# Six gather buffers in place of eight, two more kept weight units a layer, and diagonals that hold the gates ahead, in a hybrid decoder trunk on one core

## The chip, the core and the metric

The kernel runs on one core of one Trainium2 chip. It computes the whole trunk in one launch. The metric is the device time of that launch in microseconds. Before the change the median of three runs is 3154.29 us (3154.21 to 3155.14). The profile was taken of one further execution, which took 3156.79 us.

## The reference

Four layers work on 256 tokens of 1024 features in float32. The token mixers are HGRN2, FoX, Mamba-2 SSD and HGRN2 again. Behind each mixer stands a PEER expert block, which is where most of the bytes are:

```python
def peer_ffn(h, w_q, sub_keys, u_tab, v_tab):
    ...
        q = (xb @ w_q).reshape(M, PEER_HEADS, 2, PEER_HALF)
        s = jnp.einsum('mhcd,hckd->mhck', q, sub_keys).astype(jnp.float32)
        sv, si = lax.top_k(s, PEER_TOPK)
        ...
        top_s, pos = lax.top_k(cand_s, PEER_TOPK)
        idx = jnp.take_along_axis(cand_i, pos, axis=-1)
        gates = jax.nn.softmax(top_s, axis=-1)
        u = jnp.take(u_tab, idx, axis=0)
        v = jnp.take(v_tab, idx, axis=0)
        act = jax.nn.gelu(jnp.einsum('md,mhkd->mhk', xb, u).astype(jnp.float32), approximate=False) * gates
        return jnp.einsum('mhk,mhkd->md', act.astype(xb.dtype), v)
```

For each token, 8 heads choose 16 of 16384 experts each. An expert is a row `u` (dotted with the token) and a row `v` (added to the output with weight gelu(dot) times gate).

## The kernel before

The 256 tokens are two tiles of 128. A layer's expert block on one tile is a **stage**, so there are 8 stages (`STAGES`). A stage has 8 heads, a head has 8 **pairs** (`NQ`), so a stage has 64 pairs and the program 512 (`pairs`). A pair is two gathers: each brings 128 rows of `uv`, a row being 1024 values of u and 1024 of v, which is 1 MiB, into one of `NGB` buffers `GB[...]`. The two gathers of pair i are numbers 2i and 2i+1, and number n goes to `GB[n % NGB]`. In the last stage (numbers from `LAST` on) there are more buffers, the list `END`: `GB` and pieces of the memory of the weights, which are done by then.

One pair's way through the engines, in program order (the loop from L1514):

- `fetches(i)`: POOL issues gathers as indirect DMAs (L1359), as long as their row numbers are known and fewer than 2i + `NGB` are sent. A gather waits until the last reader of its buffer, TensorE's products of `NGB`/2 pairs earlier, is done.
- `dot(i, 0)`, `dot(i, 1)`: VectorE multiplies the u half with the tokens (`XR`) and sums, one number a row, into the tile `dots`.
- `spread(i)`: ScalarE computes Gelu of the two columns, multiplies each by its gate (`got[s, hh][1]`, the tile `gs`), and multiplies the mask `m64` (128 x 64, shown as `m_82`) by each result, which makes two diagonals `dg`. TensorE multiplies each diagonal with the two v halves of its buffer and adds to the accumulators `acc` (L1410): 4 calls, which are 8 matmul instructions in the trace.
- `route_steps`: VectorE, with an Exp on ScalarE, does a few steps of choosing the rows of later heads.
- `products_` and `others`: a piece of the side work `side(s)`, which is the mixer, norms and query projection of the next tile. Its calls are woven between the pairs, with costs reckoned at build time. The last of a stage's side work is drained at pair 62.

Stage s works on tile s % 2 of layer s // 2, and its side work makes ready stage s + 1. So the side work of stages 0, 2, 4, 6 is the second tile's pass over a layer, and that of 1, 3, 5 the first tile's pass over the next layer. The first pass of layer 0 runs alone ahead of the stages.

Weights come as **units** of 128 x 2048 values (1 MiB) by DMAs of SP's queue (`loads`, L354), in the order of use. Units named in `EARLY` and `LATE` have a place of their own in the memory `mix` (`place`): they are loaded for the first tile only, and the second tile finds them there. All other units are loaded for both tiles, into one of two buffers `raw` (`NRAW`). `EARLY` and `LATE` together name 11, 10, 10 and 11 units for the four layers: 42. `mix` is as long as its largest layer needs. In the lone first pass, `homes` gives some units of layer 0 a place in memory that isn't needed yet, gather buffers among it; a gather into such a buffer waits until the unit has been used.

Of the kernel before, what the change touches and what calls it, by code (L numbers as in the profile page):

```python
# [10 lines left out]
F32 = mybir.dt.float32  # L11
# [4 lines left out]
AF = mybir.ActivationFunctionType  # L16
# [3 lines left out]
P = 128  # L20
T = 256
D = 1024
# [4 lines left out]
HALF = UNIT // 2  # L27
TOPK = 16
NQ = TOPK // 2
NGB = 8  # L30
NRAW = 2
STAGES = 2 * DEPTH

KIND = ("hg", "fox", "ssd", "hg")
EARLY = {"hg": (0, 2, 4, 5, 8, 12), "fox": (0, 4, 8, 2, 10), "ssd": (0, 4, 8, 6, 29)}
LATE = {"hg": (25, 19, 21, 23, 27), "fox": (17, 19, 21, 12, 14), "ssd": (33, 35, 37, 39, 26)}
SOON = {"hg": (19, 21), "fox": (), "ssd": ()}
NEXT = {"hg": (), "fox": (12, 14), "ssd": (26,)}
# [1 line left out]
TURN = 8 * 131  # L40
MIX = max((len(EARLY[k]) + len(LATE[k])) * UNIT + MIDDLE[k] for k in MIDDLE)

# [127 lines left out]
def trunk(ctx: ExitStack, tc: tile.TileContext, d: dict, out: bass.AP):  # L170
# [4 lines left out]
    wk2 = ctx.enter_context(tc.tile_pool(name="wk2", bufs=2))  # L175
# [10 lines left out]
    sizes = (("h0", TURN), ("h1", TURN), ("xT", D), ("XR", 2 * D), ("keys", UNIT), ("SS", 2048), ("mix", MIX),  # L186
             ("gb", NGB * 2 * D))
    arena = cpool.tile([P, sum(n for _, n in sizes)], F32, name="arena")
    at_, o_ = {}, 0
# [5 lines left out]
    XR = at_["XR"].rearrange("p (g n) -> p g n", g=2)  # L195
    keys = at_["keys"].rearrange("p (g k) -> p g k", g=16)
    SS = at_["SS"].rearrange("p (h c k) -> p h c k", h=8, c=2)
    GB = [at_["gb"][:, i * 2 * D:(i + 1) * 2 * D] for i in range(NGB)]
    mix = at_["mix"]
# [17 lines left out]
    def act(o, i, f, **k):  # L217

        if f not in ghosts:
            table[0] = f  # L220
        nc.scalar.activation(o, i, f, **k)  # L221
# [15 lines left out]
    m64 = cpool.tile([P, 64], F32, name="m64")  # L237
# [13 lines left out]
    def hidden(s):  # L251

        return HB[(s - 1) % 2 if s else 0][:, 0:D]
# [5 lines left out]
    def middle(kind):  # L259

        at = [len(EARLY[kind]) * UNIT]
        most = MIX - len(LATE[kind]) * UNIT
# [8 lines left out]
    def outer(kind, t):  # L271

        at = [0 if t else MIX - len(LATE[kind]) * UNIT]
        most = len(EARLY[kind]) * UNIT if t else MIX

# [7 lines left out]
    def place(l, i):  # L283

        kind = KIND[l]
        if i in EARLY[kind]:
            o = EARLY[kind].index(i) * UNIT
        elif i in LATE[kind]:
# [5 lines left out]
    def bank():  # L294
        return psp.tile([P, 512], F32, name="ps")
# [5 lines left out]
    for l in range(DEPTH):  # L301
        nm = ("hg%d" % (l // 3), "fox", "ssm", "hg%d" % (l // 3))[l]
        n = UNITS[KIND[l] if KIND[l] != "ssd" else "ssm"]
        for t in range(2):
# [1 line left out]
            stream += [("wq%d" % l, i) for i in range(8)]  # L306
            places += [(t, l, i, place(l, i)) for i in range(n + 8)]

    homes = {1: GB[0], 3: GB[1], 6: GB[2], 7: GB[3], 9: GB[6], 10: GB[7], 11: at_["SS"], 13: at_["XR"], 16: GB[0],
             17: GB[1], 18: GB[2], 20: GB[3], 22: GB[7]}  # L310
    order = [0, 1, 2, "rest", 3, 4, 5, 6, 7, 8, 9, 10, 11, 12, 13, 14, 15, 16, 17, 18, 20, 22, "keys", "factors", 19, 21,
             24, "heads", 23, 25, "states", 26, 27]
    asked = {("early", 0), ("soon", 0), ("late", 0), ("next", 0)}
    for u in range(28, len(stream)):
        t, l, i, where = places[u]
        if where is not None and not t:
            k = KIND[l]
            token = ("early" if i in EARLY[k] else "soon" if i in SOON[k] else "next" if i in NEXT[k] else "late"), l
            if token not in asked:
# [818 lines left out]
    scored, got, routed = set(), {}, [0]  # L1138
# [206 lines left out]
    pairs = [(s, hh, q) for s, hh in heads for q in range(NQ)]  # L1345
    acts = {}
# [1 line left out]
    sent = [0]  # L1348

    LAST = 2 * NQ * 8 * (STAGES - 1)  # L1350
    END = GB + [mix[:, o:o + 2 * D] for o in range(3 * D, MIX - 2 * D + 1, 2 * D)]

    def buffer(n):

        return GB[n % NGB] if n < LAST else END[(n - LAST) % len(END)]

# [5 lines left out]
    def known(i):  # L1362

        s, hh, _ = pairs[i]
        return got[s, hh][2] if (s, hh) in got else 0

    def fetches(n):

        while sent[0] < 2 * len(pairs) and pairs[sent[0] // 2][2] < known(sent[0] // 2):
            if sent[0] - LAST >= NGB and 2 * n < LAST:  # L1370
                return
            if sent[0] >= 2 * n + (len(END) if sent[0] - LAST >= NGB else NGB):
                return
# [2 lines left out]

    def dot(i, g):
        if g == 0:
            acts[i] = wk2.tile([P, 3, 2], F32, name="dots", bufs=4)
        u = buffer(2 * i + g)[:, 0:D]  # L1380
        stt(u, u, 1.0, XR[:, g], op0=OP.mult, op1=OP.mult, accum_out=acts[i][:, 0, g:g + 1])

    def warm(n, b, x):

        for _ in range(n):
            nc.tensor.matmul(b, x[:, 0:P], x[:, 0:512], start=True, stop=True)

    def begin(s):

        accs[s] = [accp.tile([P, 512], F32, name="acc") for _ in range(2)]  # L1390
        for e in range(2):
            nc.tensor.matmul(accs[s][e], ident, hidden(s)[:, e * 512:(e + 1) * 512], start=True, stop=False)

    def spread(i):
        s, hh, q = pairs[i]
        a = acts.pop(i)
        dg = wk2.tile([P, 2, 64], F32, name="dg", bufs=4)
        act(a[:, 1], a[:, 0], AF.Gelu)
        for g in range(2):
            act(a[:, 2, g:g + 1], a[:, 1, g:g + 1], AF.Copy, scale=got[s, hh][1][:, g, 1, q:q + 1])  # L1400
        for g in range(2):
            act(dg[:, g], m64, AF.Copy, scale=a[:, 2, g:g + 1])
        if s and hh == 0 and q == 0:
            begin(s)
        if i == len(pairs) - 1:
            warm(3, bank(), cst)
        for e in range(2):
            for g in range(2):
                v = buffer(2 * i + g)[:, D + e * 512:D + (e + 1) * 512]
                nc.tensor.matmul(accs[s][e][g * 64:g * 64 + 64], dg[:, g], v, start=False,  # L1410
                                 stop=hh == 7 and q == NQ - 1)


    mixers = {"hg": hgrn, "fox": fox, "ssd": ssd}
# [75 lines left out]
    for s in range(STAGES):  # L1490
# [23 lines left out]
        for i in range(64 * s, 64 * s + 64):  # L1514
            new, end = i % 64 == 0 and s > 0, i % 64 == 63 and s + 1 < STAGES
            fetches(i)
            dot(i, 0)
            if end:
                for o, b in x[:2]:
                    nc.scalar.copy(o, b)  # L1520
            elif new:

                products_(True)
                others()
            dot(i, 1)
            spread(i)
            if end:
                (_, b), (o, c) = x[2:]
                nc.scalar.copy(x[2][0], b)
                vec.tensor_copy(o, c)  # L1530
            route_steps(3 if i > 3 else 5, i // 8 + 3)
            others()
            products_()
            if i % 64 == 62 and s + 1 < STAGES:
                while not state["done"]:
                    others()
                    products_(True)
                others()
                x = repeated()
            if table[0] is not AF.Gelu:  # L1540
                act(spare, eps, AF.Gelu)
# [20 lines left out]
```

## Time and profile before

| | before |
|---|---|
| median of three runs | 3154.29 us |
| the profiled execution | 3156.79 us |
| its span, first to last instruction | 3155.0 us |
| busy: PE, DVE, ACT, POOL | 78%, 67%, 43%, 38% of the span |
| mean granted clock of TensorE | 0.918 |
| read from HBM | 1288.38 MB |

The page gives busy times of each engine, a line with the bytes per second in 40 equal slices of the span, the DMA queues (q0 carries the gathers, q1 the weights), the chain of work that ended last, and groups of instructions by line and tile, with their number, busy time, mean duration and the idle time ahead of them. Answers of the trace add the same for a stretch of time (windows), or the instructions in order of time (timeline; in square brackets the idle time ahead of an instruction and what ended it). The 16 DMA engines' share of busy time stands behind the granted clock in a windows row.

### The profile page before, as it was taken

Reading aid. Unit: us, or ns where it says so; the run is one execution under the profiler, and the core shown is the slowest. Engines: PE = TensorE matmul, PEld = TensorE weight load, DVE = VectorE, ACT = ScalarE, POOL = GpSimd, SP = SyncE. Lnnn points to the kernel's source line nnn. Section 1 sums busy time; section 2 is a strip of 40 time slices with the busy share of each in tenths; the row PEclk is TensorE's granted clock in tenths of the full one; section 3 lists DMA queues with packets and bytes.
Section 4 is the critical chain, followed back from the end, with each engine's and each line's share of the span. In section 5 each row is a group of like instructions: output and inputs, shape, how many; then the busy total and the mean of one; then the engine's idle time right before and its main releaser. Section 6 shows DMA issues by size and latency. Waiting matters only on the chain.

```text
span 3155.0 us, 30986 instructions
## 1 busy us (share of the span) xinstructions
PE 2473.3 (78%) x8674; PEld 1104.9 (35%) x8674; DVE 2111.0 (67%) x5589; ACT 1362.1 (43%) x3911; POOL 1199.6 (38%) x1032
## 2 busy tenths in 40 slices
PE   9988787777778786888788988878767788775565
PEld 4433333333333433344233443333323333332222
DVE  2576757576676766778557887476665767577764
ACT  2344424353343533477334764245432553333332
POOL 0234334333443443333233333343433444345443
PEclk9999998988899998999889998989989998998877
DMA  8799999999999999999999999999999999999997
GB/s 338 285 421 421 421 421 411 421 420 420 411 420 420 402 421 403 422 421 421 412 418 416 418 411 408 421 418 420 421 409 421 409 419 403 421 421 421 421 422 322
DMA packets 178729, 1291.48 MB, mean 409 GB/s; under 512 B 19840, under 2 KB 20608, under 8 KB 21632
## 3 DMA queue, kind: packets, MB, share of 16 engines
q0 software_dynamic: 147456, 1073.81, 82.4%
q1 hardware_dynamic: 31104, 215.70, 16.6%
q8 instruction: 72, 1.18, 0.2%
q14 instruction: 97, 0.79, 0.1%
HBM read 1288.38 MB, written 1.05 MB: 409 GB/s over the span
## 4 chain that ended last, share of the span: by engine, by line
DMA 59%; PE 16%; DVE 12%; issue 6%; ACT 4%; POOL 2%; POOLq 0%; SPq 0%; DVEq 0%; ACTq 0%
DMA arena<-in_uv,ix 59%; DVE arena L208 9%; PE acc L1410 8%; PE pj L243 5%; PE ps L243 3%; POOL arena L1359 2%; ACT dots L221 2%; ACT L221 1%; DVE cs L208 1%; ACT dg L221 1%; ACT arena L221 1%; PE ps L247 0%; DVE si L208 0%; DVE af L208 0%; DVE sv L208 0%
## 5 line engine op out<-in xcount | busy, mean ns | idle before, releaser
L1359 POOL DMA_INDIRECT arena<-in_uv,ix x1024 | 1195.5, 1168 | 1925.6 <-PE acc L1410 1345.9
L208 DVE SCALAR_TENSOR_TENSOR arena<-arena 128x1024 f32<-128x1024 f32 (+3 forms) x1282 | 1319.9, 1048 | 827.9 <-DMA arena<-in_uv,ix 775.7
L1410 PE MATMUL acc<-arena,dg 128*64 128x512 f32 x4096 | 1255.8, 693 | 651.5 <-ACT dg L221 637.2
L1410 PEld LDWEIGHTS acc<-arena,dg 128*64 128x64 f32 x4096 | 473.9, 150 | 1258.1 <-ACT dg L221 959.9
L221 ACT ACTIVATE dots<-dots 128x2 f32<-128x2 f32 x512 | 103.3, 202 | 1563.9 <-DVE arena L208 1552.2
L243 PE MATMUL pj<-raw,arena 128*128 128x512 f32 x1144 | 554.5, 617 | 6.9 <-DMA raw<-in_fox 3.7
L221 ACT ACT_TABLE_LOAD x331 | 424.7, 1283 | 7.0 <-DVE arena L208 0.8
L243 PE MATMUL pj<-arena 128*128 128x512 f32 (+1 forms) x792 | 368.6, 602 | 3.9 <-DMA arena<-in_hg 1.7
L243 PEld LDWEIGHTS pj<-raw,arena 128*128 128x128 f32 x1144 | 204.5, 193 | 344.2 <-issue 313.4
L221 ACT ACTIVATE dg<-m,dots 128x64 f32<-128x64 f32 x1024 | 292.4, 332 | 0.0
L221 ACT ACTIVATE dots<-dots,gs 128x1 f32<-128x1 f32 x1024 | 245.6, 286 | 16.8
L243 PEld LDWEIGHTS pj<-arena 128*128 128x128 f32 x792 | 142.9, 192 | 214.0 <-issue 199.9
L243 PE MATMUL ps<-arena 128*128 128x128 f32 (+6 forms) x1088 | 139.4, 285 | 1.5 <-issue 0.8
L243 PEld LDWEIGHTS ps<-arena 128*128 128x128 f32 (+3 forms) x1088 | 113.6, 171 | 72.2 <-issue 44.4
L247 PEld LDWEIGHTS ps<-fst,arena 128*128 128x128 f32 x568 | 69.7, 149 | 83.4 <-issue 49.0
L247 PE MATMUL ps<-fst,arena 128*128 128x128 f32 x568 | 92.3, 291 | 5.6 <-ACT ig L221 3.3
L208 DVE DVE_READ_ACCUMULATOR arena<-arena 128x1 f32 x1024 | 84.2, 82 | 0.0
L221 ACT ACTIVATE arena<-arena 128x512 f32<-128x512 f32 (+3 forms) x130 | 66.4, 553 | 40.6 <-DVE arena L208 38.3
L208 DVE FIND_INDEX8 si<-sv,arena 128x8 uint32<-128x128 f32 x256 | 69.8, 285 | 0.0
L243 PE MATMUL ps<-cst,arena 128*128 128x128 f32 (+3 forms) x288 | 69.0, 367 | 0.0
L208 DVE MAX8 sv<-arena 128x8 f32<-128x128 f32 x256 | 61.6, 282 | 5.8 <-ACT arena L1177 5.7
L221 ACT ACTIVATE arena<-ps 128x512 f32<-128x512 f32 (+3 forms) x114 | 43.4, 426 | 33.1 <-PE ps L243 32.5
(122 smaller groups left out, 1259.0 us busy)
## 6 DMA issues: line engine op xcount, KB each, us to landing
raw<-in_ssm SPq DMA_DIRECT2D x52, 1024.0 KB
raw<-in_hg SPq DMA_DIRECT2D x41, 1024.0 KB
raw<-in_wq SPq DMA_DIRECT2D x32, 1024.0 KB
arena<-in_hg SPq DMA_DIRECT2D x25, 1024.0 KB
raw<-in_fox SPq DMA_DIRECT2D x18, 1024.0 KB
arena<-in_wq SPq DMA_DIRECT2D x17, 1024.0 KB
arena<-in_uv,ix POOLq DMA_INDIRECT x1024
arena<-in_fox SPq DMA_DIRECT2D x7, 1024.0 KB
```

The source lines that it names most:

```text
L208: return getattr(nc.vector, name)(o, *a, **k)
L221: nc.scalar.activation(o, i, f, **k)
L243: nc.tensor.matmul(o, w, m, start=start, stop=stop)
L247: nc.tensor.transpose(o, i, ident)
L1359: nc.gpsimd.indirect_dma_start(buffer(n), None, d["uv"], bass.IndirectOffsetOnAxis(ap=got[s, hh][0][:, g, q:q + 1], axis=0))
L1410: nc.tensor.matmul(accs[s][e][g * 64:g * 64 + 64], dg[:, g], v, start=False, stop=hh == 7 and q == NQ - 1)
```

## The change

- `NGB` goes from 8 to 6. A gather then waits for the products of 3 pairs earlier instead of 4, and `fetches` runs up to 3 pairs deep instead of 4.
- `EARLY` names two more units of each layer, so 13, 12, 12 and 13: 50. `mix` grows by two units, and the gather buffers shrink by as much.
- `homes` has 11 entries in place of 13: units 10 and 16 now have a place in `mix`, units 17, 18, 20 move by one buffer, and units 9 and 22 share `GB[5]`.
- `END` begins with the buffer that number `LAST` would have used anyway, since `LAST` isn't a multiple of 6.
- A pair's diagonals are made in two steps: `gated_diagonals(i)` writes mask times gate, and `spread(i)` multiplies that by Gelu in place. The first step is called for pair i + 1 at the end of `spread(i)`, if the gates are there. The tile `dots` loses the column for Gelu times gate.

```diff
-NGB = 8
+NGB = 6
...
-EARLY = {"hg": (0, 2, 4, 5, 8, 12), "fox": (0, 4, 8, 2, 10), "ssd": (0, 4, 8, 6, 29)}
+EARLY = {"hg": (0, 2, 4, 5, 8, 12, 16, 10), "fox": (0, 4, 8, 2, 10, 6, 15), "ssd": (0, 4, 8, 6, 29, 13, 20)}
...
-    homes = {1: GB[0], 3: GB[1], 6: GB[2], 7: GB[3], 9: GB[6], 10: GB[7], 11: at_["SS"], 13: at_["XR"], 16: GB[0],
-             17: GB[1], 18: GB[2], 20: GB[3], 22: GB[7]}
+    homes = {1: GB[0], 3: GB[1], 6: GB[2], 7: GB[3], 9: GB[5], 11: at_["SS"], 13: at_["XR"], 17: GB[0],
+             18: GB[1], 20: GB[2], 22: GB[5]}
...
-    END = GB + [mix[:, o:o + 2 * D] for o in range(3 * D, MIX - 2 * D + 1, 2 * D)]
+    END = [GB[(LAST + k) % NGB] for k in range(NGB)] + [mix[:, o:o + 2 * D] for o in range(3 * D, MIX - 2 * D + 1, 2 * D)]
...
+    def gated_diagonals(i):
+
+        s, hh, q = pairs[i]
+        dg = diags[i] = wk2.tile([P, 2, 64], F32, name="dg", bufs=4)
+        for g in range(2):
+            act(dg[:, g], m64, AF.Copy, scale=got[s, hh][1][:, g, 1, q:q + 1])
+
     def spread(i):
+
         s, hh, q = pairs[i]
         a = acts.pop(i)
-        dg = wk2.tile([P, 2, 64], F32, name="dg", bufs=4)
         act(a[:, 1], a[:, 0], AF.Gelu)
+        if i not in diags:
+            gated_diagonals(i)
+        dg = diags.pop(i)
         for g in range(2):
-            act(a[:, 2, g:g + 1], a[:, 1, g:g + 1], AF.Copy, scale=got[s, hh][1][:, g, 1, q:q + 1])
-        for g in range(2):
-            act(dg[:, g], m64, AF.Copy, scale=a[:, 2, g:g + 1])
+            act(dg[:, g], dg[:, g], AF.Copy, scale=a[:, 1, g:g + 1])
...
+        if i + 1 < len(pairs) and known(i + 1) > pairs[i + 1][2]:
+            gated_diagonals(i + 1)
```

On ScalarE, in the first pairs of stage 0 before the change (`dots` Gelu, then `dots,gs` the two gates, then `dg` the two diagonals; `ig` is the Exp of a head's routing, `spare` a dummy that brings Gelu's table back):

```order
L1148 COPY arena<-pj 128x512
L221 ACTIVATE dots<-dots 128x2
L221 ACTIVATE dots<-dots,gs 128x1 x2
L221 ACTIVATE dg<-m_82,dots 128x64 x2
L221 ACT_TABLE_LOAD
L221 ACTIVATE ig,gt<-ts,gt 128x16
L221 ACT_TABLE_LOAD
L221 ACTIVATE spare<-eps 128x1
L221 ACTIVATE dots<-dots 128x2
```

At the same place of the changed kernel:

```order
L1148 COPY arena<-pj 128x512
L221 ACTIVATE dots<-dots 128x2
L221 ACTIVATE dg<-dg,dots 128x64 x2
L221 ACTIVATE dg<-m_82,gs 128x64 x2
L221 ACT_TABLE_LOAD
L221 ACTIVATE ig,gt<-ts,gt 128x16
L221 ACT_TABLE_LOAD
L221 ACTIVATE spare<-eps 128x1
L221 ACTIVATE dots<-dots 128x2
L221 ACTIVATE dg<-dg,dots 128x64 x2
```

Gelu is now followed at once by the diagonals, and the next pair's gates stand behind them. The number of instructions stays the same. VectorE's and TensorE's orders are unchanged.

On SP's queue, where the second tile's pass over layer 0 begins (`in_x` is the second tile's input, `raw<-in_hg` that layer's units, which go through the two raw buffers; - is before, + the change):

```order
 L354 DMA arena<-in_wq 128x2048
-L1485 DMA arena<-in_x 128x1024
-L354 DMA raw<-in_hg 128x2048 x13
+L1497 DMA arena<-in_x 128x1024
+L354 DMA raw<-in_hg 128x2048 x11
 L354 DMA raw<-in_wq 128x2048 x4
 L354 DMA arena<-in_fox 128x2048
```

Two loads fall away there, and two in the second pass of each other layer. Counted over the whole queue, loads of 128 x 2048 go from 202 to 194 (four of them are keys).

More of the change, by code (lines that the diff above doesn't have):

```diff
@@ L1378, in dot @@
         if g == 0:
-            acts[i] = wk2.tile([P, 3, 2], F32, name="dots", bufs=4)
+            acts[i] = wk2.tile([P, 2, 2], F32, name="dots", bufs=4)
         u = buffer(2 * i + g)[:, 0:D]
@@ L1392, in begin @@
             nc.tensor.matmul(accs[s][e], ident, hidden(s)[:, e * 512:(e + 1) * 512], start=True, stop=False)
+    diags = {}
+    def gated_diagonals(i):
[3 more added lines that the diff above has]
+            act(dg[:, g], m64, AF.Copy, scale=got[s, hh][1][:, g, 1, q:q + 1])
     def spread(i):
```

## The prediction

> **What bounds the kernel now.** I read the page's bytes per slice first, then its queues, its chain and the gathers' group, and after that windows and the timeline.
>
> ```profile
> GB/s 338 285 421 421 421 421 411 421 420 420 411 420 420 402 421 403 422 421 421 412 418 416 418 411 408 421 418 420 421 409 421 409 419 403 421 421 421 421 422 322
> DMA packets 178729, 1291.48 MB, mean 409 GB/s; under 512 B 19840, under 2 KB 20608, under 8 KB 21632
> ...
> q0 software_dynamic: 147456, 1073.81, 82.4%
> q1 hardware_dynamic: 31104, 215.70, 16.6%
> ...
> DMA 59%; PE 16%; DVE 12%; issue 6%; ACT 4%; POOL 2%; POOLq 0%; SPq 0%; DVEq 0%; ACTq 0%
> ...
> L1359 POOL DMA_INDIRECT arena<-in_uv,ix x1024 | 1195.5, 1168 | 1925.6 <-PE acc L1410 1345.9
> ```
>
> Between start and end the slices stand at 402 to 422 GB/s, most at 420 or 421; nothing in this trace moves faster for long. The two queues together fill 99% of the 16 engines' span, and the chain that ended last is 59% gathers. So from slice 2 to slice 38 the kernel runs at the pace of its bytes. A gather is 1073.81 MB / 1024 = 1.0486 MB, at 421 GB/s **2.49 us**; a pair 4.98 us. A weight unit (128 x 2048 x 4 bytes) has the same size and the same 2.49 us. POOL waits 1345.9 us for the products that free a buffer: that wait costs nothing while other gathers are queued in the DMA engines. The change touches both, the bytes and the depth of that queue.
>
> **The weights.** Eight loads of 1 MiB fall away, two in each of the stages 0, 2, 4 and 6, all of which run at the pace of the bytes (the next row is most of stage 2). 8 x 2.49 = **19.9 us** come off.
>
> ```profile
> 970.00:1380.00 410.00, 325.24 (x1237) 152.48 (x1235) 294.93 (x822) 200.27 (x573) 161.41 (x138) 0.94 1.00 414
> ```
>
> The cover of this term is the fullness of the queue: where the engines run dry for another reason, the saved bytes save nothing.
>
> **The depth, in an ordinary stretch.** Here is one pair without weights beside it, DVE's second dot to the gather that reuses a buffer:
>
> ```profile
> 1109.15 1.23 DVE L208 SCALAR_TENSOR_TENSOR arena<-arena 128x1024 f32<-128x1024 f32 x1 [1.16 <-DMA arena<-in_uv,ix]
> ...
> 1110.41 0.20 ACT L221 ACTIVATE dots<-dots 128x2 f32<-128x2 f32 x1 [3.77 <-DVE arena L208]
> 1110.65 0.48 ACT L221 ACTIVATE dots<-dots,gs 128x1 f32<-128x1 f32 x2
> ...
> 1111.04 0.57 ACT L221 ACTIVATE dg<-m,dots 128x64 f32<-128x64 f32 x2
> ...
> 1111.42 2.17 PE L1410 MATMUL acc<-arena,dg 128*64 128x512 f32 x8
> ...
> 1113.63 0.94 POOL L1359 DMA_INDIRECT arena<-in_uv,ix  x1 [2.45 <-PE acc L1410]
> ```
>
> From the dot, which waits for the landing, to POOL's issue are 1113.63 - 1109.15 = 4.48 us. The gates stand between 1110.65 and 1111.04; the diagonals that hold them ahead take these **0.39 us** out of the way: 4.09 us are left. ScalarE itself gains nothing, by the two groups of `spread`:
>
> ```profile
> L221 ACT ACTIVATE dg<-m,dots 128x64 f32<-128x64 f32 x1024 | 292.4, 332 | 0.0
> L221 ACT ACTIVATE dots<-dots,gs 128x1 f32<-128x1 f32 x1024 | 245.6, 286 | 16.8
> ```
>
> Two instructions of 286 ns become two of 332 ns a pair, 1024 x 0.046 = 47 us more on an engine that is busy 43% of the span, behind `spread` and so while it would wait for the next dots. Without that cover it would be those 47 us. While the bytes set the pace, the earlier release is worth nothing by itself; it counts only as depth.
>
> How long an issue takes to reach a dot when nothing is queued ahead, only the first and the last gather tell:
>
> ```profile
> 114.33 1.08 POOL L1359 DMA_INDIRECT arena<-in_uv,ix  x1 [112.64 <-DVE arena L208]
> ...
> 115.00:116.00 1.00, 1.00 (x19) 0.83 (x16) 0.93 (x5) 0.35 (x1) 0.69 (x2) 1.00 0.00 0
> 116.00:117.00 1.00, 1.00 (x3) 0.52 (x4) 0.93 (x4) 0.24 (x1) 0.70 (x2) 1.00 0.77 139
> 117.00:118.00 1.00, 0.85 (x2) 0.02 (x1) 0.93 (x6) 0.00 (x0) 0.90 (x1) 1.00 0.87 336
> ...
> 3142.50:3143.00 0.50, 0.50 (x3) 0.00 (x0) 0.00 (x0) 0.00 (x0) 0.00 (x0) 0.50 0.04 16
> 3143.00:3143.50 0.50, 0.50 (x2) 0.00 (x0) 0.00 (x0) 0.00 (x0) 0.00 (x0) 0.50 0.00 0
> ...
> 3143.55 1.23 DVE L208 SCALAR_TENSOR_TENSOR arena<-arena 128x1024 f32<-128x1024 f32 x1 [1.14 <-DMA arena<-in_uv,ix]
> ```
>
> Bytes flow some 2.0 us after the issue begins, and a dot starts some 0.6 us after the last bytes. The loop of a buffer pair is then 4.09 + 2.0 + 4.98 (its two gathers) + 0.6 = 11.7 us. With six buffers it has to fit into the time of three pairs, 14.95 us: a **margin of 3.3 us**. With eight it was 4.48 + 2.0 + 4.98 + 0.6 = 12.1 against 19.9 us, a margin of 7.9 us. So in an ordinary stretch six buffers keep the queue full, and the term is nothing. A weight unit in the queue adds 2.49 us of margin while it is there.
>
> The Trainium skill, "DMA: Bandwidth & Descriptors", section "Anatomy of one DMA — SWDGE (gpsimd) path", fits one DMA as 2.0 us plus bytes / 436 GB/s. By that a lone gather would be an estimate of 4.4 us, where the rows above give 2.0 + 2.49 + 0.6 = 5.1 us; the margin would be 4.0 us, the forecast the same, and the slower rival below (1.4 us over the margin) would pay 0.7 us a head, 9.8 us in all. The rows decide.
>
> **The depth, where the release runs late.** These windows lie at four of the seven later stage starts, in the SSD mixer and near the end of the weights:
>
> ```profile
> 870.00:892.00 22.00, 16.12 (x105) 8.47 (x101) 14.78 (x39) 7.99 (x28) 9.98 (x9) 0.95 1.01 424
> 1240.00:1262.00 22.00, 16.62 (x102) 8.87 (x98) 18.18 (x55) 11.32 (x34) 9.48 (x9) 0.90 0.91 358
> 1655.00:1677.00 22.00, 16.83 (x108) 9.11 (x104) 17.29 (x50) 10.40 (x33) 8.92 (x9) 0.95 1.00 408
> 1868.00:1912.00 44.00, 40.69 (x167) 20.34 (x166) 37.73 (x92) 29.15 (x64) 16.80 (x14) 0.92 0.96 381
> 2632.00:2660.00 28.00, 27.91 (x110) 12.49 (x106) 18.92 (x50) 6.88 (x27) 11.68 (x10) 0.79 0.91 371
> 2820.00:2845.00 25.00, 16.91 (x104) 9.11 (x101) 20.24 (x59) 8.10 (x30) 15.68 (x13) 0.97 1.01 420
> ```
>
> Three of them fall short even with eight buffers (358, 381 and 371 GB/s): the engines are late there by more than 7.9 us, and the DMA engines run dry. With two buffers fewer they run dry two gathers sooner, so each such place costs up to 4.98 us more, and down to nothing if weights fill the hole. Of the nine places (seven stage starts and the two in the mixers) the other starts shown hold 408 to 424 GB/s. I count the two places at a share of 0.91 whole, since their queue is the nearest to empty already, and the others with nothing: 2 x 4.98 = **10.0 us**. The ends are 0 and 9 x 4.98 = 44.8 us.
>
> **The start.** Unit 22 now lies in the sixth buffer, not the eighth:
>
> ```profile
> 120.07 0.33 SPq L1485 DMA_DIRECT2D arena<-in_x  x1
> ...
> 121.96 0.94 POOL L1359 DMA_INDIRECT arena<-in_uv,ix  x1 [0.30 <-issue]
> 129.78 1.69 POOL L1359 DMA_INDIRECT arena<-in_uv,ix  x1 [6.88 <-PE pj L243]
> ```
>
> The eighth gather waits for that unit's use until 129.78; now the sixth does. Five gathers and half a MiB of input are 5.5 x 2.49 = 13.7 us of bytes; 475 KB (1.1 us) are through by 118, so they end near 130.6, and new bytes come at 129.78 + 2.0 = 131.8. That is **1.2 us** dry (0 to the whole 6.88). Unit 16, loaded sooner, changes nothing there, since the first gather waits for DVE (114.33, above). At the very end the last pair has no gates in its way: 0.4 us less. In the last stage both kernels have 18 buffers.
>
> **Sum.** 3156.79 - 19.9 + 10.0 + 1.2 - 0.4 = 3147.7 us for the profiled execution; it is 2.5 us over the median, so **3145.2 us**.
>
> **Rivals.** *Given back at the nine places.* The three short places pay 4.98 us each and the six others 1 us each: 20.9 in place of 10.0, so 3156 us, no change that can be told. For it: a stage start at 0.91 shows how late the release comes there. Against it: the other starts at 1.00 and 1.01.
>
> *Slower: a late release at many heads.* Each head's routing puts an Exp on ScalarE:
>
> ```profile
> L221 ACT ACT_TABLE_LOAD x331 | 424.7, 1283 | 7.0 <-DVE arena L208 0.8
> ...
> 1100.00:1125.00 25.00, 19.77 (x56) 7.92 (x56) 17.97 (x52) 9.35 (x34) 10.13 (x9) 0.93 1.01 420
> ...
> 1116.39 2.17 PE L1410 MATMUL acc<-arena,dg 128*64 128x512 f32 x8 [0.88 <-ACT dg L221]
> ...
> 1121.37 3.80 PE L1410 MATMUL acc<-arena,dg 128*64 128x512 f32 x8 [2.81 <-ACT dg L221]
> 1121.57 1.28 ACT L221 ACT_TABLE_LOAD   x1
> 1122.87 0.31 ACT L221 ACTIVATE ig<-ts,gt 128x16 f32<-128x16 f32 x1
> ...
> 1124.51 1.28 ACT L221 ACT_TABLE_LOAD   x1
> 1125.81 0.20 ACT L221 ACTIVATE spare<-eps 128x1 f32<-128x1 f32 x1
> ```
>
> Two table loads, Exp and dummy are 1.28 + 0.31 + 1.28 + 0.20 = 3.1 us ahead of a Gelu that happens to be ready; and the products took 3.80 in place of 2.17 us behind a pause of 2.81 us, 1.6 more. Together 4.7 us, 1.4 over the margin of 3.3. If both meet in 7 of the 56 heads of the first seven stages, the gain of 9.1 us is gone; at 11 the kernel is slower by 0.2%. At a quarter of them, 14, it costs 19.6 us: **3165 us**. For it: the 331 table loads, some 41 a stage. Against it: here the next dots came only after the tables, and the stretch, with both, moved 420 GB/s (with eight buffers).
>
> The Trainium skill, "TensorE: Matmul & The Clock Gate", section "HAM oscillation — how this bites in real kernels", says that idle gaps of TensorE over about 3.4 us bring its clock down. Each dry spell would then bring slower products behind it, at the 1.6 us of the rows above 9 x 1.6 = 14 us for the nine places, 3160 us; the trace shows slow products already behind a pause of 2.81 us, so it agrees in kind, not in the length. I take that as part of this rival.
>
> *It doesn't do what it says:* excluded, since SP's queue has 194 loads in place of 202.
>
> **Chances.** Faster by over 0.2% (6.3 us, about what a measurement of this kernel can tell): 0.43, the forecast. Within it: 0.33, the first rival. Slower: 0.24, the second. The lowest the terms allow is 3154.3 - 20.3 = 3134; with all nine places and the start's whole wait it is 3186. I take 3136 to 3172, which leaves out a little of the slower rival and the very best case.
>
> **What would show it.** 1283.1 MB in all; ordinary slices still at 420; the release 0.39 us shorter and the group `dots<-dots,gs` gone; the three short windows shorter still, by two gathers at most. Wrong would be: slices of 400 and less in ordinary stretches, or DVE's waits for gathers (775.7 us below) rising by far more than 10 us.
>
> ```profile
> DVE arena L208 <- DMA arena<-in_uv,ix: 775.7, 515, 4.7
> ```

## The result and the profile after

The changed kernel takes **3190.89 us** (median of 6 runs, 3178.27 to 3196.00), the kernel before 3154.25 us beside it (6 runs, 3153.02 to 3156.03). The ratio is 1.0108, 95% interval 1.0089 to 1.0127: slower by 1.1%, where 3145.2 us and a range of 3136 to 3172 were predicted. The profiled execution is one of the quicker ones, 3180.63 us with a span of 3178.9.

The page of the changed kernel, the lines that answer to those of before (bytes per slice, packets, second queue, chain, the gathers' group and the two groups of `spread`):

```profile
GB/s 339 287 408 413 411 414 392 420 414 417 410 403 412 396 413 397 422 408 420 412 416 397 405 407 417 413 403 417 413 408 417 398 403 400 405 405 422 421 422 348
DMA packets 177576, 1283.09 MB, mean 404 GB/s; under 512 B 19712, under 2 KB 20480, under 8 KB 21504
...
q1 hardware_dynamic: 29952, 207.31, 15.8%
...
DMA 56%; PE 16%; DVE 13%; issue 8%; ACT 4%; POOL 3%; POOLq 0%; SPq 0%; DVEq 0%; ACTq 0%
...
L1359 POOL DMA_INDIRECT arena<-in_uv,ix x1024 | 1230.7, 1202 | 1914.7 <-PE acc L1420 1378.4
...
L221 ACT ACTIVATE dg<-dg,dots 128x64 f32<-128x64 f32 x1024 | 300.5, 340 | 16.7
...
L221 ACT ACTIVATE dg<-m,gs 128x64 f32<-128x64 f32 x1024 | 292.6, 333 | 0.0
```

The bytes fell as predicted, by 8.39 MB, all of them in the second queue, and the gates left the way. But the slices that stood at 420 or 421 now stand at 392 to 420 in nearly every place from the third slice on, until the last stage returns to 421. The loss is not at a few places.

The GB/s line can be turned into time. A slice that moves x GB/s where 421 would be possible loses (1 - x/421) of its length. Over the third to the 36th slice (78.9 us each before, 79.5 after) that makes 28.3 us before and 77.0 after: **48.7 us more**. I call this the loss against 421; it is used for every kernel below. The last slice went from 322 to 348, a loss of 18.6 and now 13.8, so 4.8 us less. With the bytes: 48.7 - 19.9 - 4.8 = 24.0 us, and the spans differ by 3178.9 - 3155.0 = 23.9. So the two profiled executions are accounted for: one term, the depth, was taken at 10 and is 49.

The same windows as in the prediction, now of the changed kernel:

```profile
870.00:892.00 22.00, 16.03 (x101) 8.76 (x100) 14.54 (x38) 7.30 (x24) 10.30 (x10) 0.88 1.00 409
970.00:1380.00 410.00, 321.59 (x1209) 150.40 (x1207) 285.00 (x792) 197.19 (x550) 161.17 (x136) 0.92 1.00 408
1240.00:1262.00 22.00, 15.67 (x96) 8.82 (x98) 16.55 (x53) 10.43 (x30) 7.87 (x7) 0.84 0.97 387
1655.00:1677.00 22.00, 15.66 (x97) 9.26 (x95) 14.26 (x35) 9.47 (x28) 8.65 (x8) 0.81 0.99 400
1868.00:1912.00 44.00, 40.82 (x194) 21.11 (x192) 37.04 (x96) 35.17 (x77) 13.73 (x13) 0.96 0.99 394
2632.00:2660.00 28.00, 20.53 (x74) 9.23 (x74) 19.74 (x52) 14.00 (x37) 8.93 (x8) 0.94 1.01 417
2820.00:2845.00 25.00, 18.46 (x74) 9.24 (x75) 19.08 (x56) 11.23 (x34) 9.61 (x10) 0.86 1.01 409
```

The work has moved by some microseconds against these windows, so the three short ones can't be compared one by one. What they show is that the places that were full before (424, 408, 420) are now as thin as the rest, and that the long stretch of stage 2 lost 6 GB/s **at an unchanged DMA share of 1.00**. A dry queue shows here mostly as packets that take long: in the trace a packet of 8192 bytes usually takes 313 ns, and those over 400 ns exceed it by some 23.5 us a DMA engine before and by some 62 after. Of the 38 more, 4 to 5 lie at the first four pairs of the stages, depending on where the cut between two pairs is made; the rest is spread over all other pairs of stages 0 to 6. The other 10 us of the 48.7 are not in long packets: over the same slices the packets' mean share of the 16 engines' time fell from 1.009 to 1.002 (they overlap a little, so it can pass 1).

One such place, in no way special (timeline of the changed kernel; one pair's second dot, its products, POOL's two issues that they release, and the dot on the gather that was issued last before):

```profile
1689.80 1.23 DVE L208 SCALAR_TENSOR_TENSOR arena<-arena 128x1024 f32<-128x1024 f32 x1 [1.21 <-DMA arena<-in_uv,ix]
...
1691.70 3.91 PE L1420 MATMUL acc<-arena,dg 128*64 128x512 f32 x8 [3.93 <-ACT dg L221]
...
1695.65 1.60 POOL L1359 DMA_INDIRECT arena<-in_uv,ix  x1 [5.02 <-PE acc L1420]
...
1697.55 1.04 POOL L1359 DMA_INDIRECT arena<-in_uv,ix  x1 [0.30 <-DVE ti L208]
...
1700.14 1.22 DVE L208 SCALAR_TENSOR_TENSOR arena<-arena 128x1024 f32<-128x1024 f32 x1
```

The bytes at the same place, in windows of 1 us (the last three columns are TensorE's granted clock, the DMA share and GB/s):

```profile
1697.00:1698.00 1.00, 0.88 (x2) 0.53 (x4) 0.90 (x7) 0.98 (x5) 0.69 (x2) 0.50 1.08 434
1698.00:1699.00 1.00, 1.00 (x5) 0.58 (x3) 1.00 (x3) 1.00 (x1) 0.59 (x1) 0.50 0.92 262
1699.00:1700.00 1.00, 1.00 (x6) 0.34 (x2) 1.00 (x2) 0.97 (x4) 0.00 (x0) 0.50 0.89 344
1700.00:1701.00 1.00, 1.00 (x4) 0.04 (x1) 0.86 (x3) 0.99 (x2) 0.00 (x0) 0.50 0.97 377
```

Behind a pause of 3.93 us the products took 3.91 us at half clock, so the issue came 5.85 us after the dot, where 4.09 is the least. It ended at 1697.25, and the gather ahead of it had landed when its dot began at 1700.14: it was issued 2.9 us ahead of the queue's end. By the prediction's working that is ample, since bytes follow some 1 us after the end of an issue. Yet the bytes fall to 262 GB/s from 1698 on, two microseconds before the queue's end. The trace has 16 landings for a gather, one from each DMA engine, and the first of them for the gather ahead is at 1698.22: the bytes fall when the first engine is done.

That distance, from the end of the issue of a pair's first gather to the landing of the gather ahead of it, is called the **lead** below. It is worked out from the trace for the 444 pairs from the fifth one to the end of stage 6; where a trace lacks some of a gather's 16 landings, the last one that it has is taken. Lead and loss are those of the one profiled execution, the time is the median of all runs:

| kernel | buffers, units, gates | pairs with a lead under 6.5 us | lead, tenth percentile, us | loss against 421, us | time, us |
|---|---|---|---|---|---|
| before | 8, 42, late | 8 | 7.9 | 28.3 | 3154.3 |
| changed | 6, 50, ahead | 296 | 2.9 | 77.0 | 3190.9 |

Sorted by lead, the changed kernel's pairs between 2.5 and 6.5 us have 0.17 us of long packets each (291 pairs, 50 us), those over 6.5 us have 0.06. So two theories. **Lead:** the queue begins to run dry at a lead of some 4.5 to 6.5 us, not of 1 to 1.5 as by the prediction's working, so that six buffers are short in ordinary stretches too. **Slow products:** the products at half clock (97 of the first 448 pairs took over 2.5 us, 84 before) make single releases late, and only there is anything lost. The rival to both is the prediction's own count, the nine late places.

### The profile page after: what moved, and what is told of

The parts are those of the page before. It is cut to its first block, busy times and chain, and to the rows that moved or that the text cites. A ratio compares the mean times of both kernels' runs of the same rounds, so it can differ in the third digit from the quotient of the medians.

```text
span 3178.9 us, 30842 instructions
## 1 busy us (share of the span) xinstructions
PE 2489.8 (78%) x8674; PEld 1108.9 (35%) x8674; DVE 2112.4 (66%) x5589; ACT 1415.3 (45%) x3911; POOL 1234.7 (39%) x1032
## 4 chain that ended last, share of the span: by engine, by line
DMA 56%; PE 16%; DVE 13%; issue 8%; ACT 4%; POOL 3%; POOLq 0%; SPq 0%; DVEq 0%; ACTq 0%
DMA arena<-in_uv,ix 56%; DVE arena L208 10%; PE acc L1420 8%; PE pj L243 5%; POOL arena L1359 3%; PE ps L243 3%; ACT dg L221 1%; ACT L221 1%; DVE cs L208 1%; ACT arena L221 1%; ACT dots L221 1%; DVE si L208 0%; DVE af L208 0%; PE ps L247 0%; DVE ti L208 0%
## 5 line engine op out<-in xcount | busy, mean ns | idle before, releaser
L1359 POOL DMA_INDIRECT arena<-in_uv,ix x1024 | 1230.7, 1202 | 1914.7 <-PE acc L1420 1378.4
L1420 PE MATMUL acc<-arena,dg 128*64 128x512 f32 x4096 | 1275.1, 705 | 654.7 <-ACT dg L221 652.5
L1420 PEld LDWEIGHTS acc<-arena,dg 128*64 128x64 f32 x4096 | 481.3, 152 | 1265.5 <-ACT dg L221 995.3
L243 PE MATMUL pj<-raw,arena 128*128 128x512 f32 x1032 | 501.0, 618 | 6.6 <-DMA raw<-in_ssm 6.0
L243 PE MATMUL pj<-arena 128*128 128x512 f32 (+1 forms) x904 | 424.9, 606 | 4.1 <-ACT arena L695 2.0
L221 ACT ACTIVATE dg<-dg,dots 128x64 f32<-128x64 f32 x1024 | 300.5, 340 | 16.7
L243 PEld LDWEIGHTS pj<-raw,arena 128*128 128x128 f32 x1032 | 184.7, 193 | 311.2 <-issue 285.5
L221 ACT ACTIVATE dg<-m,gs 128x64 f32<-128x64 f32 x1024 | 292.6, 333 | 0.0
L243 PEld LDWEIGHTS pj<-arena 128*128 128x128 f32 x904 | 164.2, 194 | 253.8 <-issue 232.1
```

Of the source, the lines that this page charges most:

```text
L243: nc.tensor.matmul(o, w, m, start=start, stop=stop)
L1359: nc.gpsimd.indirect_dma_start(buffer(n), None, d["uv"], bass.IndirectOffsetOnAxis(ap=got[s, hh][0][:, g, q:q + 1], axis=0))
```

## Experiments

Where a ratio stands, it is against the kernel before on the same chip, with its 95% interval.

### Each part alone

The gates ahead with eight buffers and 42 units (`spread`, `gated_diagonals` and `dots` as in the change, nothing else):

> The kernel before with the diagonals that hold the gates ahead, nothing else: eight buffers, 42 units. Two theories on the changed kernel's extra time. Depth: two buffers fewer let the DMA queue run dry in ordinary stretches, all over the program; then this part alone, with eight buffers, does nothing, 3152 to 3156 us (0.9995 to 1.0005 of before), the release 0.39 us sooner and the slices as before. ScalarE: the longer diagonals (47 us more ScalarE work, behind the spread and ahead of the routing's Exp and the next Gelu) are what costs; then this kernel is slower by most of the 37 us that the changed kernel lost and its missing gain of 20, 3175 us or more.

Measured: 3153.84 us (11 runs), 0.9996 (0.9987 to 1.0005); loss 27.0 us. The gates ahead do nothing that can be told where eight buffers hold the queue, and the longer ScalarE work does no harm. DVE's waits for gathers rose in this kernel from 775.7 to 803.8 us without any loss of time: my sign "these waits rise by far more than 10 us" was a bad one: they rose where nothing was lost.

The depth alone, six of the eight buffers of the kernel before:

```diff
+USED = 6
...
-        return GB[n % NGB] if n < LAST else END[(n - LAST) % len(END)]
+        return GB[n % USED] if n < LAST else END[(n - LAST) % len(END)]
...
-            if sent[0] >= 2 * n + (len(END) if sent[0] - LAST >= NGB else NGB):
+            if sent[0] >= 2 * n + (len(END) if sent[0] - LAST >= USED else USED):
```

> The kernel before with gathers into six of its eight buffers, 42 units, diagonals as before: the depth alone, with the release 0.39 us later than in the changed kernel. Depth theory: 3215 to 3240 us, the changed kernel's 3191 plus up to 19.9 for eight units plus 0.39 us at each of its some 74 dry spells (29 us), and DVE's waits for gathers above the changed kernel's 835.7 us. The prediction's count, only the nine late places: 3154 + 10 + some 4, 3165 to 3170 us. Nothing from depth: 3154 us.

Measured: 3225.63 us (5 runs), 1.0221 (1.0207 to 1.0235). The same with the gates ahead, so the changed kernel with 42 units:

> The same six of eight buffers and 42 units, with the gates ahead: the changed kernel without its eight weight units, so that the distance between the two is what the units' bytes are worth. If the bytes count in full beside the dry spells: 3191 + 19.9 = 3211 us. If a weight unit in the queue covers a dry spell: 3195 to 3205 us, since then units that go also take cover away. The prediction's count: 3165 us.

Measured: 3205.84 us (5 runs, 3185.61 to 3213.12), 1.0143 (1.0118 to 1.0168). Bytes per slice with six buffers and the gates late:

```profile
GB/s 336 285 407 421 405 417 391 418 399 414 411 386 410 381 408 397 417 414 420 413 412 398 416 417 405 416 385 400 414 408 406 386 389 406 411 392 416 421 421 359
```

And with the gates ahead:

```profile
GB/s 338 285 412 415 412 414 389 421 402 406 412 385 409 391 406 397 411 416 418 409 412 398 418 418 403 411 379 408 419 415 406 397 412 414 412 403 422 422 421 350
```

So at equal bytes two buffers cost 3205.84 - 3153.84 = **52 us** with the gates ahead by the medians (46 by the ratios, since the six-buffer runs scatter by 28 us) and 71 without, all over the program: the nine places are out as the main cause. The gates ahead, 0.39 us a release, are worth 19.8 us at six buffers, with intervals apart, and 1.1 at eight, within the interval; 19.8 / 0.39 = 51, as if about one pair in nine passed its whole delay on to the end. Between six buffers with 42 and with 50 units are 15 us by the medians, 11 by the ratios, with intervals that overlap: whether the eight units still give the whole 19.9 where the queue is dry isn't settled.

### The first buffer sooner

The changed kernel with the loops of the products turned:

```diff
-        for e in range(2):
-            for g in range(2):
+        for g in range(2):
+            for e in range(2):
```

> The changed kernel with the loops of the products turned, so that the pair's first buffer is done after half of them (some 1.1 us sooner at full clock, 1.9 us at half). The first of the two gathers that wait is then issued earlier; the same instructions run. Depth theory (a lead short by one or two us at some 74 places, all over the program): 15 to 25 us less than the changed kernel, 3166 to 3176 us, with fewer slices under 418 GB/s. Nine late places alone: at most 9 x 1.9 = 17 us of the holes, but more likely 5, since those releases are late by many us, 3186 us. If the time comes from something other than the release (homes, loads that collide): 3191 us.

Measured: 3191.65 us (4 runs), 1.0111 (1.0095 to 1.0126). This missed the 3166 to 3176 of the depth theory, because the edit doesn't release anything sooner. The timeline of one pair, its products and the issue that they release:

```profile
1119.87 1.96 PE L1420 MATMUL acc<-arena,dg 128*64 128x512 f32 x8
...
1122.08 0.94 POOL L1359 DMA_INDIRECT arena<-in_uv,ix  x1 [2.28 <-PE acc L1420]
```

The products' group on the same kernel's page (busy us, then the mean ns of one instruction):

```profile
L1420 PE MATMUL acc<-arena,dg 128*64 128x512 f32 x4096 | 1278.1, 708 | 661.1 <-ACT dg L221 658.2
```

By the program's order the issue needs only half of the products, and still it comes 2.2 us after their start, which is also the median in the changed kernel. The trace shows why. In both kernels only the seventh and the eighth of the eight instructions report that they are done, 1.95 and 2.18 us after the first one starts, and in the kernel with the turned loops the second instruction already waits for the second gather. So the instructions of the two buffers alternate in both, and neither buffer is reported done at half time. (The 708 ns are modelled ends; the instructions start some 0.24 us apart.) The run says nothing on lead or products.

### Slow products

The changed kernel with one extra matmul at 114 pairs, those where TensorE was idle when the second gather landed (`IDLE` lists them from the trace):

```diff
+        if i in IDLE:
+            warm(1, bank(), buffer(2 * i + 1)[:, D:2 * D])
         a = acts.pop(i)
```

> The changed kernel with one more 128x512 matmul of TensorE, into a PS bank that nobody reads, ahead of the products at 114 pairs: those whose trace shows TensorE free before, or 0.2 us after, the pair's second gather landed (in the trace some 80 of the 97 pairs whose products took over 2.5 us are among them). It reads the second gather's v half, so it runs between the landing and the products and is done before them. Slow products theory (TensorE's clock drops in the pause, the products take 3.8 in place of 2.2 us, and the release that is 1.6 us late is what dries the queue): the products over 2.5 us go from 97 to 30 or fewer, and most of the 37 us of dry spells go: 3155 to 3170 us. Depth alone (the lead is too short at a release on time as well, the slow products only add to it): 3180 to 3187 us. If the clock doesn't come back in so short a time: 3191 us, the products unchanged.

Measured: 3177.87 us (5 runs), 1.0087 (1.0072 to 1.0103); loss 64.1 us in place of 77.0. Its products' group and the extra ones:

```profile
L1429 PE MATMUL acc<-arena,dg 128*64 128x512 f32 x4096 | 1225.4, 680 | 435.3 <-ACT dg L221 430.9
...
L1386 PE MATMUL ps<-arena 128*128 128x512 f32 x228 | 140.1, 699 | 132.0 <-DMA arena<-in_uv,ix 128.6
```

Products over 2.5 us went from 97 to 66, not to 30; most of the slow products stay behind one extra matmul. The time fell by 13 us by the medians and by 7 by the ratios, whose intervals overlap; the profiled loss fell by 12.9, in the quickest of its executions (3169.04 us). So slow products are probably a part of the loss, but how large a part isn't settled; the slow products theory asked for 3155 to 3170 and didn't get it. Another run, below, puts them in their place.

### Seven buffers

Seven of the eight buffers, 42 units, gates ahead (`USED = 7`):

> Gathers into seven of eight buffers, 42 units, gates ahead: the middle between eight (3154 us) and six (3206 us) buffers at the same bytes. A pair's first gather then waits for the products of four pairs earlier, as with eight, and the second for those of three pairs earlier; the queue's lead is one gather, 2.49 us, longer than with six. If the queue needs a lead of some 4.5 us (six: 2.5 to 3 us in ordinary stretches): 3155 to 3162 us. If the cost is even in the buffers: 3180 us.

Measured: 3155.83 us (11 runs), 1.0001 (0.9992 to 1.0010). Seven cost 2 us against eight, within the interval, and six 52: no even price, an edge between them. The edge is used by a kernel with seven buffers, 46 units (one more a layer) and the gates ahead:

```diff
-NGB = 6
+NGB = 7
-EARLY = {"hg": (0, 2, 4, 5, 8, 12, 16, 10), "fox": (0, 4, 8, 2, 10, 6, 15), "ssd": (0, 4, 8, 6, 29, 13, 20)}
+EARLY = {"hg": (0, 2, 4, 5, 8, 12, 10), "fox": (0, 4, 8, 2, 10, 6), "ssd": (0, 4, 8, 6, 29, 13)}
...
```

(`homes` moves along: unit 16 has a buffer again, and unit 22 goes to the seventh.)

> Seven buffers with the memory of one for one more unit a layer, 46 in place of 42, gates ahead. If seven buffers hold the queue, four units of 2.49 us come off, less what the seventh's shorter lead costs: 3144 to 3152 us, faster than both kernels. If the cost is even in the buffers: 3180 - 10 = 3170 us.

Measured: **3145.73 us** (9 runs, 3142.64 to 3148.30), 0.9971 (0.9961 to 0.9981): faster than both kernels. Bytes per slice of seven buffers with 42 units:

```profile
GB/s 338 285 421 421 421 418 407 421 421 421 411 410 421 412 421 407 422 420 420 415 414 413 421 407 410 421 418 414 420 413 422 413 421 398 421 421 421 421 421 345
```

And with 46:

```profile
GB/s 340 279 421 421 421 418 407 421 421 421 413 418 421 407 421 408 422 416 420 417 411 408 415 421 415 419 407 421 419 417 422 401 421 419 419 420 422 421 421 338
```

Where the queue stays full, four units are worth 10.1 us, 2.5 each, just their bytes. The same kernel with the 114 extra matmuls, and with the diagonals of before:

> The same seven buffers and 46 units with the 114 extra matmuls. Slow products theory: 2 to 6 us less than without them, 3142 to 3148 us. If seven buffers have lead enough, no difference to them: within 2 us.

> Seven buffers and 46 units with the diagonals of before, so that every release is 0.39 us later than in the kernel with seven buffers and the gates ahead (3145.7 us). With eight buffers those 0.39 us were worth nothing (1.1 us), with six 20 us. Lead theory: with seven the queue's lead is over 6.5 us at nine pairs in ten, so they are worth little, 0 to 5 us: 3145 to 3151 us. If each release costs at seven as at six: 3165 us.

Measured: 3146.69 us (6 runs), 0.9971 (0.9959 to 0.9983), and 3147.60 us (11 runs), 0.9976 (0.9967 to 0.9985). With the extra matmuls slow products fell from 90 to 60 and the time not at all; releases later by 0.39 us cost 1.9 us, within the intervals. So neither delay costs anything that can be told while the lead is there. That is how the two theories stand to each other: at seven buffers half-clock products cost nothing by themselves; where they cost something, they do it by eating a lead that six buffers don't have.

### The lead shortened in another way

Does the number of buffers matter, or only the lead? GpSimd clears the freed buffer before it issues a pair's first gather, with seven and with eight buffers:

```diff
+            if USED <= sent[0] < LAST and sent[0] % 2 == 0:
+                for _ in range(1):
+                    nc.gpsimd.memset(buffer(sent[0]), 0.0)
+                    nc.gpsimd.memset(buffer(sent[0])[:, 0:512], 0.0)
             fetch(sent[0])
```

(This is the kernel with seven; with eight, `NGB` stands for `USED`, and the double delay has `range(2)`.)

> Seven of eight buffers, 42 units, gates ahead, and each pair's first gather issued late on purpose: GpSimd first clears the freed buffer (128x2048 and 128x512 again), which by the trace's 0.96 us for 128x1024 is some 2.4 us, about one gather's 2.49 us, and puts the queue's lead where six buffers have it. The same bytes, the same order elsewhere. Lead theory (what six buffers lose is the time by which the next gather is issued ahead of the queue's end, whatever makes it short): 3195 to 3215 us, as with six buffers and 42 units (3206 us). If it is the number of buffers or gathers in flight itself, and not the lead: 3156 us, as without the delay. If the delay only hits the late releases: some 3165 us.

> Eight buffers, 42 units, gates ahead, with the same delay of some 2.4 us ahead of each pair's first gather: by the lead theory as good as seven buffers without it, 3153 to 3162 us. If a release that is later by 2.4 us costs by itself: the same rise as at seven buffers, 3195 us or more.

> Eight buffers with twice the delay, some 4.8 us ahead of each pair's first gather, which is about what the two missing buffers took from the lead: by the lead theory 3195 to 3225 us. If depth as such decides: 3154 us. GpSimd is busy for some 80% of the time then, so that a part over 3206 us may be the delay's own doing.

Measured, in this order: 3202.87 us (4 runs), 1.0151 (1.0132 to 1.0170); 3180.79 us (4 runs), 1.0082 (1.0065 to 1.0099); 3887.16 us (4 runs), 1.2333 (1.2312 to 1.2354). The page of the eight buffers with one delay, its bytes per slice and GpSimd's groups:

```profile
GB/s 337 288 410 421 421 417 381 421 420 419 413 395 421 382 413 420 398 421 421 420 410 387 421 421 406 421 413 421 421 419 421 377 421 421 414 409 421 421 421 345
...
L1359 POOL DMA_INDIRECT arena<-in_uv,ix x1024 | 1170.3, 1143 | 545.0 <-DVE arena L208 151.3 <-issue 96.5 <-POOL arena L1377 87.3
L1376 POOL MEMSET arena<- 128x2048 f32 x444 | 805.6, 1814 | 366.5 <-PE acc L1424 364.9
L1377 POOL MEMSET arena<- 128x512 f32 x444 | 233.9, 527 | 25.6
```

And the clearing's group with two delays:

```profile
L1376 POOL MEMSET arena<- 128x2048 f32 x888 | 1610.9, 1814 | 28.1 <-PE acc L1424 2.2
```

Seven buffers came out as the lead theory says. Eight didn't: 3153 to 3162 was expected. The delay was longer than one gather, and the trace shows why: the least time from a landing to the issue that reuses the buffer grew by 2.45 us, but its median by 3.7, since GpSimd works in order and the next clearing stands behind the last issue. With two delays the run missed its 3195 to 3225 by far: GpSimd became the bound (its clearing waits for TensorE 2.2 us in all, and clearing and issues fill 83% of the span), so that run tells nothing on the lead. The other two can be set beside the rest. All kernels with 42 units in order of time, and three with more units below them; lead and loss are again those of the profiled execution:

| buffers, units, what else | pairs with a lead under 6.5 us | lead, tenth percentile, us | loss against 421, us | time, us |
|---|---|---|---|---|
| 8, 42, gates ahead | 4 | 8.4 | 27.0 | 3153.8 |
| 7, 42, gates ahead | 21 | 6.7 | 29.4 | 3155.8 |
| 8, 42, gates ahead, delay | 137 | 4.2 | 56.1 | 3180.8 |
| 7, 42, gates ahead, delay | 188 | 3.6 | 77.0 | 3202.9 |
| 6, 42, gates ahead | 275 | 2.9 | 88.5 | 3205.8 |
| 6, 42, gates late | 297 | 2.9 | 100.3 | 3225.6 |
| 7, 46, gates ahead | 25 | 6.6 | 27.1 | 3145.7 |
| 6, 50, gates ahead, 114 matmuls | 292 | 2.9 (3.8 over the pairs with all landings) | 64.1 | 3177.9 |
| 6, 50, gates ahead (the change) | 296 | 2.9 | 77.0 | 3190.9 |

At equal bytes the time rises with the number of short leads, whichever way they were shortened; eight buffers with short leads lose, seven with long ones don't. The order is all that this shows: among the six-buffer kernels the tenth percentile hardly differs, and the loss does. A rival for the two rows with the delay is the clearing itself, which writes to the same memory as the gathers. The trace speaks against it: with eight buffers and the delay every pair's first gather has a clearing ahead of it, but the 307 pairs with a lead over 6.5 us have 0.02 us of long packets each, and the 137 others 0.28. One reserve: the clearing also made DVE's small copies slower (`gs<-ig` from 197 to 280 ns), so a little of those two rows may be that.

## Why the prediction was wrong

- **The bytes.** Right: 8.39 MB. Their 2.49 us a unit come off in full where the queue is full (2.5 us at seven buffers); at six buffers 11 to 15 us of the 19.9 were measured, with too wide an interval to say whether something is lost.
- **The depth, in an ordinary stretch.** This is the step that failed, the "margin of 3.3 us" and its "the term is nothing". It cost most of the 49 us, and 46 to 52 us at equal bytes. The working let the next bytes flow 2.0 us after an issue starts, which is some 1 us after it ends, and put 0.6 us between the last bytes and the dot, so a lead of some 1.5 us would do. By that criterion hardly a pair ran dry: 99 of 100 had a lead of 2.5 us or more. The runs show that the loss begins between a tenth percentile of 6.7 us (nothing) and 4.2 (27 us). What the first and last gather of the program show, one gather with nothing around it, is not what a queue needs to run at full pace.
- **One pair as the measure.** The 4.48 us from dot to issue was a good median (4.46 to the products' end), but a quarter of the pairs before took 5.86 and more, a tenth 6.25. Less the 0.39 us of the gates, that alone would have left a margin of 1.9 and 1.5 us; together with the lead it did not.
- **The depth at the late places.** Counted at 10.0 us. The first four pairs of the stages got 4 to 5 us more of long packets, so this term was not too small, and is a small part.
- **The start.** Counted at 1.2 us, and nothing of it shows: the sixth gather was issued at 123.13, not at 129.78, and the first two slices moved 339 and 287 GB/s after 338 and 285.
- **The gates ahead.** The release got 0.38 us shorter in the trace (least time from landing to the products' end, 4.47 to 4.09). That it is worth nothing while the bytes set the pace held at eight and seven buffers (1.1 and 1.9 us, within the intervals). At six the bytes no longer set the pace everywhere, and it is worth 19.8 us.
- **The rivals.** The slower one had the sign, and slow products are in it as I put it, but its price (14 heads at 1.4 us) assumed the 3.3 us margin and so stayed 26 us short. "Given back at the nine places" named the wrong places. The Trainium skill's fit of one DMA, 2.0 us plus bytes / 436 GB/s ("DMA: Bandwidth & Descriptors", section "Anatomy of one DMA — SWDGE (gpsimd) path"), would have given a margin of 4.0 us and failed in the same way: it is the latency of one transfer, and the runs show that a stream of them needs a longer lead.

Why the lead has to be so long is in part in the traces. A gather lands on 16 DMA engines, and from the first of them to the last it takes 6.9 us in the median with eight buffers and the gates ahead, 3.7 with seven and 2.2 with six. The engine that is done first runs dry first, and the lead above is counted to the one that is done last. Here the lead is counted to the first instead, for the pairs' first gathers whose 16 landings are all in the trace. Each field has the number of pairs and the mean long packets of a pair, per engine, from 0.5 us before the first landing to 1 us after the last:

| kernel | to the first landing: under 1.5 us | 1.5 to 2.5 | 2.5 to 3.5 | over 3.5 | to the last landing: 5 to 6.5 | 6.5 to 8 |
|---|---|---|---|---|---|---|
| before (8) | 18, 0.59 us | 44, 0.18 | 63, 0.08 | 259, 0.02 | 2, 0.41 | 50, 0.19 |
| 8, 42, gates ahead, delay | 36, 0.48 us | 69, 0.25 | 50, 0.03 | 288, 0.01 | 60, 0.11 | 80, 0.01 |
| 6, 50, gates ahead (the change) | 66, 0.40 us | 93, 0.19 | 82, 0.03 | 203, 0.01 | 108, 0.02 | 76, 0.01 |

Counted to the last engine, the lead at which packets get long differs from kernel to kernel; counted to the first, it is some 2.5 us in all three. So the margin was reckoned to the wrong engine: at six buffers the first one is done 2.2 us ahead of the last, and the next gather must be issued some 2.5 us ahead of that. This is read off the traces; no run moved this spread of the engines alone, and why it is 2.5 us and not the working's 1.5 stays open.

## What to carry to other kernels

Where a kernel runs at the pace of its transfers, a buffer is worth what it adds to the lead at which the next transfer is issued, and that has an edge: find it by using fewer of the buffers that are there, a change of one number, before memory is moved elsewhere. Take the lead from its distribution over all transfers, count it to the first DMA engine that is done, and don't set it against the latency of a lone transfer. And judge by bytes per slice: the share of busy DMA stayed at 1.00 while the rate fell, and VectorE's waits for gathers rose where no time was lost (803.8 us with eight buffers and the gates ahead) and fell where 27 us were (724.9 with the delay).

## What was not expected of the hardware

- A DMA engine that runs dry hardly shows as idle: at a share of 0.89 to 0.97 the core moved 262 to 377 GB/s (windows above), while single packets took 400 to 2200 ns in place of 313.
- The 16 DMA engines drift apart, and the further the longer the leads are (6.9, 3.7 and 2.2 us, above; 3.2 with eight buffers and the delay). At the end of the program that costs: from the first to the last landing of the very last gather are 9.6 us before and 4.7 after, and the last slice moved 322 and 348 GB/s.
- TensorE's clock falls behind shorter pauses than I had thought. In the changed kernel products over 2.8 us came behind none of 64 pauses under 0.5 us, 11 of 87 between 1 and 2, 18 of 25 between 2.0 and 2.5, 5 of 13 between 2.5 and 2.75, 18 of 20 between 2.75 and 3.0, and 30 of 32 over 3.5. So the length of the last pause alone doesn't decide it. The Trainium skill, "TensorE: Matmul & The Clock Gate", section "HAM oscillation — how this bites in real kernels", puts the pauses that do harm at over some 3.4 us; here the measurement decides, and from some 2 us on they often do.
